# Layer-norm means on TensorE: one float32 product each, or two float32r products of an exact split

## The chip, the core and the metric

One of the cores of a Trainium2 chip runs the whole kernel, as one program in one launch. The metric is the device time of the execution in microseconds; the median of several runs counts. The engines are TensorE (PE in the profile; PEld is its weight load), VectorE (DVE), ScalarE (ACT), GpSimd (POOL) and SyncE (SP), which issues the DMAs.

## What is computed

One layer of a streaming encoder over 1024 prompt frames and 32 sample frames, 1056 columns of 1024 channels in all. Cut to the part that the change touches:

```python
def _layer_norm(x, g, b):
    mu = jnp.mean(xf, axis=-1, keepdims=True)
    var = jnp.mean(jnp.square(xf - mu), axis=-1, keepdims=True)
    y = (xf - mu) * lax.rsqrt(var + LN_EPS) * g + b
...
    mix = jnp.einsum('btd,de->bte', g_conv * y_conv + g_attn * y_attn, w_o)
    x1 = _layer_norm(DN_ALPHA * x + mix, ln1_g, ln1_b)
    h = jnp.square(jax.nn.relu(jnp.einsum('btd,df->btf', x1, w_up)))
    return _layer_norm(DN_ALPHA * x1 + jnp.einsum('btf,fd->btd', h, w_down), ln2_g, ln2_b)
```

Before these come a combined input projection, a convolution branch and an attention branch; their results and caches are outputs too.

## The kernel before

Channels lie on the 128 partitions, frames on the free axis, so the residual stream is eight tiles `acc[0..7]` of 128 x 1056, and a sum over channels is a sum over eight tiles followed by a sum over partitions. All large products run in float32r with operands that were split into two parts, hi and lo: a term is hi x hi + hi x lo + lo x hi, three products. A split is a Copy to float32r on ACT (hi) and a subtraction on DVE (lo).

**The norms.** `run_sum` adds the eight tiles of a block on DVE as they come. `norm_steps` (L1222) then takes the sum through the partitions with one product on PE whose weights are `mean_d`, a 128 x 128 tile filled with 1/1024 (L560); as both operands are float32 it is a float32 product. DVE subtracts the mean from each tile, ACT squares it, DVE adds the squares up (`squares`, L1200), and a second product with `mean_d` gives the variance. ACT takes the root, DVE the reciprocal, and `emit` writes each tile.

**Where they run.** The first norm (x1, behind w_o) is made in four blocks of 264 columns. The w_o products run in three groups: blocks 0 and 2, then block 1, then block 3 (`GROUPS`, L66). Its results, split into `x_0h`, `x_0l` to `x_3h`, `x_3l`, are what the first up-projection products read, in the order of blocks 0, 2, 1, 3 (`ORDER`, L67), four groups of 24 products for each block; inside a group the eight channel tiles are read one after the other, three products for each. Ahead of a block's first group `I.finish` (L1427) puts out what is left of its norm. The second norm (behind the down projection) is made in blocks of 384, 384 and 288 columns (`TAIL`, L63). The last block has a path of its own at the end of the kernel (L1790 on): it subtracts an estimate of the mean, the mean of its first tile times eight (`ps_mu_last`, copied by ACT to `lnpart`), as soon as that is there, while the other products run, and corrects it at the end; its products with `mean_d` are float32.

**What sets the order.** PE, DVE, ACT and POOL run their instructions in the order in which the program writes them. A planner (`class Issue`, L83) keeps an estimated clock for each engine while the program is written. After every six products of a large term, `service` (L127) looks at a list of background streams, the norms among them; each stream is a generator that yields what its next step needs, and it goes on when that is due by the clock of PE. A need with a number ahead of it, `(margin, need)`, is due that many ns after the need is ready; `NMARGIN` is 2000 (L73). A callable is due when it gives true: `yield lambda: nth < 2 or turned[nth - 2]` holds a norm back until the norm two before it has emitted its last tile. `("dve", "act", LAG)` lets a stream run at most 1 us ahead of PE.

```python
        margin = NMARGIN
        yield (margin, need)
        yield lambda: nth < 2 or turned[nth - 2]
        mu = cbank(f"mu_{tag}", "mu", 2)[:, :n]
        mean(mu, [s])
...
        yield (margin, [total])
        mean(var, [total])
```

Names in the trace: `lnsum_n` the sum, `lnsq_n` the squares, `lnvar_n` their sum, `ps_mu_n` and `ps_var_n` the two products, `rstd_n` the root and its reciprocal; `ps_o`, `ps_up` and `ps_dn` are the products of w_o, of the up projection and of the down projection. `spp` is the split of a hidden tile in the same stretch.

Of the kernel before, what the change touches and what calls it, by code (L numbers as in the profile page):

```python
# [9 lines left out]
F32 = mybir.dt.float32  # L10
F32R = mybir.dt.float32r
BF16 = mybir.dt.bfloat16
AF = mybir.ActivationFunctionType
# [4 lines left out]
P = 128  # L18
D = 1024
# [43 lines left out]
TAIL = (384, 384, 288)  # L63
CB = T // 4
# [18 lines left out]
class Issue:  # L83
# [121 lines left out]
    def mm(self, ps, w, x, start, stop):  # L205
        n = self.size(ps)
        self.run("pe", 122 if n == CB else max(107, n / 2.36) if x.dtype != F32 else max(430, n * 1.71), [ps], [w, x])
        self.nc.tensor.matmul(ps, lhsT=w, rhs=x, start=start, stop=stop)  # L208
# [5 lines left out]
    def act(self, out, in_, func, bias=None, **kw):  # L214
        aps = [] if bias is None else [bias]
        self.run("act", self.size(in_) * 0.81 + (62 if self.psum(in_) else 103) + 93 * len(aps),
                 [out] + [v for k, v in kw.items() if k == "accum_out"], [in_] + aps)
        if bias is not None:
            kw["bias"] = bias
        self.nc.scalar.activation(out, in_, func, **kw)  # L220
# [5 lines left out]
    def tt(self, out, a, b, op, eng="dve"):  # L226
        n = self.size(out)
        self.run(eng, n * 1.01 + 80 if eng == "dve" else n * 1.97 + 150, [out], [a, b])
        (self.nc.vector if eng == "dve" else self.nc.gpsimd).tensor_tensor(out, a, b, op)  # L229
# [31 lines left out]
def col(t, k):  # L261
    return t[:, k * P:(k + 1) * P]


def f32(t):
    return t.bitcast(F32)
# [3 lines left out]
def hybrid_layer(ctx: ExitStack, tc, io):  # L270
    nc = tc.nc
    I = Issue(nc)
    dma, mm, act, cp, tt, ts, stt = I.dma, I.mm, I.act, I.cp, I.tt, I.ts, I.stt
    ADD, SUB, MUL, MAX, MIN = ALU.add, ALU.subtract, ALU.mult, ALU.max, ALU.min

    @contextmanager
    def pool(name, **kw):
        with tc.tile_pool(name=name, bufs=1, reuse_waits="tile", **kw) as p:
            yield Slots(I, p)

    ctx.enter_context(tc.manual_schedule(engines={mybir.EngineType.PE, mybir.EngineType.DVE, mybir.EngineType.Activation, mybir.EngineType.Pool}))
    const = ctx.enter_context(pool("const"))
# [151 lines left out]
    def mm3(ps, terms, late=False, low=False):  # L434

        order = [(0, i, j) for i in range(len(terms)) for j in range(3)]
        if late:
            order.sort(key=lambda o: o[2] == 2)
        if low:
            order.sort(key=lambda o: o[2] == 1)  # L440
        n = len(order)
        for s, (_, i, j) in enumerate(order):
            wh, wl, xh, xl = terms[i]
            mm(ps, wl if j == 2 else wh, xl if j == 1 else xh, s == 0, s == n - 1)
            if s % (8 if low else 6) == (7 if low else 5) and s < n - 1:
                yield False
        yield True

    def dense(ps, terms, late=False):
        for _ in mm3(ps, terms, late):  # L450
            I.service()


    xp = ctx.enter_context(pool("x"))

# [39 lines left out]
    with pool("conv") as pv_, pool("a") as pa, pool("pa", space=PSUM) as psa:  # L495
# [61 lines left out]
        nc.gpsimd.memset(ones, 1.0)  # L557
        mean_c = pv_.tile([P, P], F32, name="mean_c")
        nc.gpsimd.memset(mean_c, 1.0 / C_CONV)
        mean_d = const.tile([P, P], F32, name="mean_d")  # L560
        nc.gpsimd.memset(mean_d, 1.0 / D)
        zt = pa.tile([P, 9, H], F32, name="zt")
        nc.gpsimd.memset(zt, 0.0)
        cum = pa.tile([P, 16, H], F32, name="cum")
# [179 lines left out]
        for half in range(2):  # L744
            ws = [W.take() for g in range(2)]
            for t in range(9):
                tk = slice(t * P, (t + 1) * P) if t < 8 else slice(T - P, T)
                ps = bank("v")[:, :VW]
# [6 lines left out]
                ps = ps[P - r:P, :]  # L755
# [20 lines left out]
        for m in range(4):  # L776
            for name in "qk":
                w = W.take()
                for c in range(NCH):
                    ps = bank(name)[:, :CH]  # L780
                    dense(ps, on_x(w, c))
                    a = pa.tile([P, CH], F32, tag="qk32", bufs=2, name=f"{name}32_{m}_{c}")
# [375 lines left out]
    pc = ctx.enter_context(pool("c"))  # L1158
    cblocks = [slice(b * CB, (b + 1) * CB) for b in range(NB)]
    num = [0]  # L1160
    bank_pool, ln_pool = [None], [None]

    def cbank(name, tag="acc", bufs=5):
        num[0] += 1
        return bank_pool[0].tile([P, 512], F32, tag=tag, bufs=bufs, name=f"ps_{name}_{num[0]}")
# [15 lines left out]
            return self.at(0, k), self.at(1, k)  # L1181

    def tmp(tag, bufs, name):
        return ln_pool[0].tile([P, LNW], F32, tag=tag, bufs=bufs, name=name)

    def run_sum(cs, m, s, tag, eng="dve"):

# [12 lines left out]
    def squares(sq, t, total, nth, n, tag):  # L1200

        m = len(sq)
        q = tmp(f"lnsq{nth % 2}", LNQ, f"lnsq{m}_{tag}")[:, :n]
        act(q, t, AF.Square)
        sq.append(q)
        if m == 2:
            total = tmp("lnvar", 2, f"lnvar_{tag}")[:, :n]
            tt(total, sq[0], sq[1], ADD)
        elif m > 2:
            tt(total, total, sq[m - 1], ADD)  # L1210
        return total

    def mean(ps, parts):
        for i, a in enumerate(parts):
            mm(ps, mean_d, a, i == 0, i == len(parts) - 1)
# [6 lines left out]
    def norm_steps(cs, tag, s, emit, need, nth):  # L1222
        n = cs.stop - cs.start
        tiles = [a[:, cs] for a in acc]
        margin = NMARGIN
        yield (margin, need)
        yield lambda: nth < 2 or turned[nth - 2]
        mu = cbank(f"mu_{tag}", "mu", 2)[:, :n]
        mean(mu, [s])
        var = cbank(f"var_{tag}", "var", 1)[:, :n]  # L1230
        total, sq = None, []
        for m, t in enumerate(tiles):
            tt(t, t, mu, SUB)
            total = squares(sq, t, total, nth, n, tag)
            if m % 2:
                yield ("dve", "act", LAG)
        tt(total, total, sq[-1], ADD)
        yield (margin, [total])
        mean(var, [total])
        rstd = tmp("lnrstd", 2, f"rstd_{tag}")[:, :n]  # L1240
        act(rstd, var, AF.Sqrt, bias=eps)
        I.recip(rstd, rstd)
        for m in range(KD):
            emit(m, rstd, tiles)
            turned[nth] = m == KD - 1
            yield ("dve", "act", LAG)

    with pool("ps1", space=PSUM) as bank_pool[0]:
        yo = [cbank("yo", "mu", 2)[:, :CB]]
        with pool("y") as py:  # L1250
# [27 lines left out]
            for n, (m, b) in enumerate(order):  # L1278
                if b == 0 and 0 < m < KD - 2:
                    load_gates(m + 2, py, 2)  # L1280
                while first and len(ahead) < (5 if n < YM * NB else 1):
# [3 lines left out]
                    ps = cbank("yc")[:, :CB]  # L1285
                    dense(ps, y_part(0, fm, cblocks[fb]))
                    ahead.append(ps)
                ps = yo.pop() if yo else cbank("yo", "mu", 2)[:, :CB]
# [18 lines left out]
        W.limit, W.engine = NPLAN, "dve"  # L1307
        S.pool = ctx_s.enter_context(pool("s", side="right"))
        with pool("l1") as ln_pool[0]:
            LNW, LNQ = CB, 2  # L1310
            for n, m in enumerate(m for m in range(0, KD, 2) if m not in WO_AGAIN):
                kept[NWO + m] = lambda n=n, m=m: [ln_pool[0].tile([P, T], F32R, tag=f"d{n}", bufs=2, name=f"{x}_wo{m}") for x in ("whi", "wlo")]
            xrs = []
# [56 lines left out]
            for group in GROUPS:  # L1370
                sums = {}
                for m in range(KD):
                    again = m in wk
                    w = wk[m] if again else W.take()
                    for b in group:
                        load_x(taken + 2)
                        taken += 1
                        ps = cbank("o")[:, :CB]
# [45 lines left out]
            for n, (f, b) in enumerate(order):  # L1424
# [9 lines left out]
                ps = cbank("up")[:, :CB]  # L1434
# [77 lines left out]
    with pool("ps2", space=PSUM) as psd:  # L1512
# [64 lines left out]
        for p in PAIRS:  # L1577
# [9 lines left out]
            ps = go(4)  # L1587
# [94 lines left out]
        for kb in range(NKB):  # L1682
            if kb == 1:
                extra = between()
            for g in range(2):
# [3 lines left out]
                for i in range(7):  # L1689
# [12 lines left out]
                    for n in range(2):  # L1702
                        q = 2 * g + n
                        ps = product(f"d{i}", [[(col(wh, 2 * n + f), col(wl, 2 * n + f), u[s][:, 2 * f * CB:(2 * f + 1) * CB],
                                                 u[s][:, (2 * f + 1) * CB:(2 * f + 2) * CB]) for f in range(2)] for s in range(2)])
# [22 lines left out]

    bank_pool[0] = ctx.enter_context(pool("ps3", space=PSUM))
    ln_pool[0] = ctx.enter_context(pool("l2"))  # L1730
    LNW, LNQ = max(TAIL), 3
    W.limit = len(plan)

    def output(cs, new=False):
# [45 lines left out]
    for i, cs in enumerate(tail):  # L1780
# [11 lines left out]
        n, s = cs.stop - cs.start, None  # L1792
        for m in range(KD):
            ps = more(m)
            a = acc[m][:, cs]
            tt(a, ps, a, ADD)
            s = run_sum(cs, m, s, f"n2_{i}")
# [4 lines left out]
    n, tag = cs.stop - cs.start, "n2_last"  # L1802
    tiles = [a[:, cs] for a in acc]
    nth, sq, var, s, held_ps = len(turned), [], None, None, {}
# [12 lines left out]
    for m in range(KD):  # L1817
        held_ps[m] = more(m)
        if m == 0:
            tt(tiles[0], held_ps.pop(0), tiles[0], ADD)  # L1820
            mu = cbank("mu_last", "mu", 2)[:, :n]
            part = spare("lnpart")
        if m == KM:
# [4 lines left out]
            s = spare("lnsum2")  # L1828
# [11 lines left out]
    ps = cbank("var_last", "var", 1)[:, :n]  # L1840
# [95 lines left out]
```

## Time and profile before

| | us |
|---|---|
| median of 3 runs | 1450.78 |
| lowest, highest | 1450.74, 1450.80 |
| the profiled execution | 1450.36 |
| its span, first to last instruction | 1448.6 |
| PE busy in the span | 1429.2 (99%) |
| DVE busy | 1122.0 (77%) |
| ACT busy | 678.8 (47%) |
| POOL busy | 127.0 (9%) |
| mean granted clock of TensorE | 0.995 of full speed |

The profile is of one execution, and its own time stands beside its span. An engine's busy share is a mean over stages with different limits, so what a change in one stage is worth is read from that stage: from the chain of work that ended last, and from the idle time ahead of an instruction with what ended it, which the timeline shows in brackets. PE's matmuls overlap: a row's duration is longer than the time by which it moves the next one, and that time is read from the chain or from the distance of starts.

### The profile page before, as it was taken

How to read it: one execution, taken by the hardware profiler on the slowest of the kernel's cores; microseconds unless marked ns; L12 is line 12 of the kernel's file. 1: busy time of each engine (PE TensorE's matmuls, PEld its weight loads, DVE VectorE, ACT ScalarE, POOL GpSimd, SP SyncE). 2: the span in 40 equal slices, each digit the busy share in tenths (PEclk: the TensorE clock that was granted, in tenths of full speed). 3: DMA queues.
4: the chain of work that ended last, by engine and by line, in shares of the span. 5: the costliest groups of instructions: out<-in, count | busy, mean ns of one | idle time of the engine just before them, and what ended most of it. 6: DMA issues, size and time to landing. Idle time of an engine off the chain costs nothing.

```text
span 1448.6 us, 28009 instructions
## 1 busy us (share of the span) xinstructions
PE 1429.2 (99%) x10639; PEld 1406.0 (97%) x10639; DVE 1122.0 (77%) x1926; ACT 678.8 (47%) x1426; POOL 127.0 (9%) x186
## 2 busy tenths in 40 slices
PE   9999999999999999999999999999999999999995
PEld 8999999999999999999999999999999999999994
DVE  6999899865666655856697889888985799879767
ACT  5113333455666656533345666666656332222224
POOL 0000000023455533000000000000000000000001
PEclk9999999999999999999999999999999999999997
DMA  7125554278455557426233347676689888884112
GB/s 247 46 61 160 165 171 159 90 244 234 111 150 157 153 153 263 147 78 195 86 127 128 133 171 281 237 253 239 229 301 335 331 315 313 295 314 161 46 44 77
DMA packets 157442, 267.91 MB, mean 185 GB/s; under 512 B 22680, under 2 KB 81272, under 8 KB 157308
## 3 DMA queue, kind: packets, MB, share of 16 engines
q1 hardware_dynamic: 156764, 264.54, 55.1%
q0 software_dynamic: 544, 1.59, 0.5%
q8 instruction: 84, 1.38, 0.4%
q14 instruction: 50, 0.41, 0.1%
HBM read 168.29 MB, written 97.74 MB: 184 GB/s over the span
## 4 chain that ended last, share of the span: by engine, by line
PE 96%; DVE 2%; ACT 1%; DMA 0%; issue 0%; SPq 0%; ACTq 0%; DVEq 0%
PE ps_u L208 18%; PE ps_d L208 17%; PE ps_g L208 13%; PE ps_o L208 6%; PE ps_dn L208 6%; PE ps_up L208 5%; PE ps_v L208 4%; PE ps_yc L208 3%; PE ps_k L208 3%; PE ps_glua L208 3%; PE ps_q L208 3%; PE ps_glub L208 3%; PE ps_yo L208 3%; PE ps_s L208 3%; PE ps_pv L208 2%; PE ps_tr L212 2%
## 5 line engine op out<-in xcount | busy, mean ns | idle before, releaser
L237 DVE SCALAR_TENSOR_TENSOR ca<-u,prm,ca 128x1086 f32<-128x1086 f32 x120 | 161.8, 1348 | 2.4
L208 PE MATMUL ps_g<-xh,whi 128*128 128x352 f32 x384 | 131.8, 343 | 0.0
L220 ACT ACTIVATE swhi<-s 128x512 fp32r<-128x512 f32 x100 | 61.9, 624 | 147.2 <-DVE s L229 140.7
L208 PE MATMUL ps_g<-xh,wlo 128*128 128x352 f32 x384 | 123.8, 322 | 0.0
L208 PE MATMUL ps_g<-xl,whi 128*128 128x352 f32 x384 | 121.5, 322 | 0.0
L208 PE MATMUL ps_u<-tl,swhi 128*128 128x264 f32 x416 | 118.4, 285 | 0.0
L208 PE MATMUL ps_u<-th,swhi 128*128 128x264 f32 x416 | 118.2, 284 | 0.0
L208 PE MATMUL ps_u<-th,swlo 128*128 128x264 f32 x416 | 118.2, 284 | 0.0
L220 ACT ACTIVATE whi<-raw 128x512 fp32r<-128x512 f32 (+1 forms) x120 | 69.7, 625 | 71.8 <-PE ps_glua L208 21.8
L229 DVE TENSOR_TENSOR tl<-ps_tr,th 128x512 fp32r<-128x512 f32 (+2 forms) x96 | 51.5, 553 | 60.1 <-ACT th L220 59.4
L208 PE MATMUL ps_d<-hu_h,swhi 128*128 128x264 f32 x480 | 93.0, 285 | 0.0
L208 PE MATMUL ps_d<-hu_l,swhi 128*128 128x264 f32 x480 | 92.8, 285 | 0.0
L220 ACT ACTIVATE r<-r 128x528 f32<-128x528 f32 (+1 forms) x120 | 73.9, 616 | 38.2 <-DVE r L229 35.9
L229 DVE TENSOR_TENSOR r<-r,ps_u 128x528 f32<-128x528 f32 x91 | 62.8, 702 | 29.9 <-PE ps_u L208 29.9
L229 DVE TENSOR_TENSOR wlo<-raw,whi 128x512 fp32r<-128x512 f32 (+1 forms) x100 | 64.8, 688 | 26.7 <-ACT whi L220 25.1
L229 POOL TENSOR_TENSOR acc<-acc,lnrest 128x288 f32<-128x288 f32 x5 | 3.8, 788 | 860.6 <-DVE lnvar_n_last L229 860.6
L208 PEld LDWEIGHTS ps_u<-th,swhi 128*128 128x128 f32 x416 | 78.3, 188 | 0.0
L208 PEld LDWEIGHTS ps_u<-th,swlo 128*128 128x128 f32 x416 | 78.3, 188 | 0.0
L208 PEld LDWEIGHTS ps_u<-tl,swhi 128*128 128x128 f32 x416 | 78.2, 188 | 0.0
L208 PEld LDWEIGHTS ps_d<-hu_h,swhi 128*128 128x128 f32 x480 | 74.6, 189 | 0.3 <-issue 0.2
L208 PEld LDWEIGHTS ps_d<-hu_l,swhi 128*128 128x128 f32 x480 | 74.6, 189 | 0.0
L208 PEld LDWEIGHTS ps_g<-xh,whi 128*128 128x128 f32 x384 | 72.7, 189 | 0.8
(423 smaller groups left out, 5008.7 us busy)
## 6 DMA issues: line engine op xcount, KB each, us to landing
h_s<-sp SPq DMA_DIRECT2D x84, 528.0 KB
raw<-in_w_in_dram SPq DMA_DIRECT2D x64, 256.0 KB
hu_h<-h_s SPq DMA_DIRECT2D x30, 528.0 KB
hu_l<-h_s SPq DMA_DIRECT2D x30, 528.0 KB
sraw<-in_w_up_dram SPq DMA_DIRECT2D x52, 256.0 KB
hu<-h_s SPq DMA_DIRECT2D x24, 528.0 KB
sraw<-in_w_ds_dram SPq DMA_DIRECT2D x48, 256.0 KB
g_s<-gt SPq DMA_DIRECT2D x48, 176.0 KB
```

Source lines behind the costliest of these rows:

```text
L208: self.nc.tensor.matmul(ps, lhsT=w, rhs=x, start=start, stop=stop)
L212: self.nc.tensor.transpose(ps, x, ident)
L220: self.nc.scalar.activation(out, in_, func, **kw)
L229: (self.nc.vector if eng == "dve" else self.nc.gpsimd).tensor_tensor(out, a, b, op)
L237: self.nc.vector.scalar_tensor_tensor(out, a, s, b, op0, op1)
```

## The change

Each sum is split in two before its product: hi is the sum rounded to float32r (a Copy on ACT), lo the rest (a subtraction on DVE). The mean is then two float32r products with the same weights, accumulated in one bank. The weights tile becomes float32r, `mean_r`, and `mean_d` is the same tile read as float32. The parts take slots of the tag of the squares. The wait for the sum comes without a margin now, the split follows, and the margin stands behind the parts. This holds for the norms that go through `norm_steps`: four blocks of the first norm and two of the second; the last block is as before.

```diff
+    def two_parts(src, pool, nth, tag):
+        n = src.shape[-1]
+        parts = [pool.tile([P, LNW[0]], F32R, tag=f"lnsq{nth % 2}", bufs=LNQ[0], name=f"ln{x}_{tag}")[:, :n] for x in "hl"]
+        act(parts[0], src, AF.Copy)
+        tt(parts[1], src, f32(parts[0]), SUB)
+        return parts
+
+    def mean_of(ps, share, parts):
+        for i, a in enumerate(parts):
+            mm(ps, share, a, i == 0, i == len(parts) - 1)
...
-        mean_d = const.tile([P, P], F32, name="mean_d")
-        nc.gpsimd.memset(mean_d, 1.0 / D)
+        mean_r = const.tile([P, P], F32R, name="mean_r")
+        nc.gpsimd.memset(f32(mean_r), 1.0 / D)
+        mean_d = f32(mean_r)
...
-        yield (margin, need)
+        yield need
         yield lambda: nth < 2 or turned[nth - 2]
+        parts = two_parts(s, ln_pool[0], nth, f"mu_{tag}")
+        yield (margin, parts)
         mu = cbank(f"mu_{tag}", "mu", 2)[:, :n]
-        mean(mu, [s])
+        mean_of(mu, mean_r, parts)
...
         tt(total, total, sq[-1], ADD)
-        yield (margin, [total])
-        mean(var, [total])
+        parts = two_parts(total, ln_pool[0], nth, f"var_{tag}")
+        yield (margin, parts)
+        mean_of(var, mean_r, parts)
```

The rest of the diff turns the width and the number of buffers of these tiles, `LNW` and `LNQ`, into one-element lists, with the same values.

## Rows read from the trace of the kernel before

**Rows 1.** The page, parts 1 and 4: busy shares, and the chain by engine.

```profile
PE 1429.2 (99%) x10639; PEld 1406.0 (97%) x10639; DVE 1122.0 (77%) x1926; ACT 678.8 (47%) x1426; POOL 127.0 (9%) x186
...
PE 96%; DVE 2%; ACT 1%; DMA 0%; issue 0%; SPq 0%; ACTq 0%; DVEq 0%
```

**Rows 2.** Waits of PE over the span, the longest: total, times, longest (us).

```profile
PE ps_md_last L208 <- DVE acc L229: 2.8, 1, 2.8
```

**Rows 3.** Chain in order of time, two stretches: start, length (us), what.

```profile
701.68 0.45 PE ps_mu_n L208 x2
...
702.12 2.91 PE ps_o L208 x24
...
1371.22 0.65 PE ps_mu_n L208 x2
...
1371.87 12.59 PE ps_dn L208 x72
```

**Rows 4.** Instructions that read mean_d: ns min/median/max, first and last start.

```profile
L208 PE MATMUL ps_mu_n<-lnsum_n,mean_d x12: 384/386/486, 701.5 to 1406.1; 128*128 128x264 f32 x8, 128*128 128x384 f32 x4
```

**Rows 5.** Instructions on spp, a split of the same width: ns min/median/max.

```profile
L220 ACT ACTIVATE spp<-r x20: 423/426/635, 763.4 to 1075.2; 128x264 fp32r<-128x264 f32 x16, 128x528 fp32r<-128x528 f32 x4
...
L229 DVE TENSOR_TENSOR spp<-r,spp x20: 426/431/711, 771.4 to 1078.6; 128x264 fp32r<-128x264 f32 x16, 128x528 fp32r<-128x528 f32 x4
```

**Rows 6.** Timeline of DVE, w_o and first w_up products: start, length (us).

```profile
701.44 0.43 DVE L229 TENSOR_TENSOR lnsum_n<-lnsum_n,acc 128x264 f32<-128x264 f32 x1
...
702.16 1.11 DVE L229 TENSOR_TENSOR acc<-acc,ps_mu_n 128x264 f32<-128x264 f32 x3 [0.28 <-PE ps_mu_n L208]
...
717.51 1.80 DVE L241 RECIPROCAL rstd_n<-rstd_n 128x264 f32<-128x264 f32 x1 [1.20 <-ACT rstd_n L220]
...
774.85 1.80 DVE L241 RECIPROCAL rstd_n<-rstd_n 128x264 f32<-128x264 f32 x1 [3.05 <-ACT rstd_n L220]
...
783.36 0.49 DVE L237 SCALAR_TENSOR_TENSOR x_3l<-acc,prm,x_3h 128x264 fp32r<-128x264 f32 x1 [0.18 <-ACT x_3h L220]
...
790.90 1.29 DVE L229 TENSOR_TENSOR wlo<-raw,whi 128x512 fp32r<-128x512 f32 x2 [4.76 <-ACT whi L220]
```

**Rows 7.** Timeline of ACT, same stretch.

```profile
715.70 1.28 ACT L220 ACT_TABLE_LOAD   x1
```

**Rows 8.** Timeline of PE, same stretch.

```profile
701.52 0.61 PE L208 MATMUL ps_mu_n<-lnsum_n,mean_d 128*128 128x264 f32 x2
...
785.78 0.28 PE L208 MATMUL ps_up<-x_3h,whi 128*128 128x264 f32 x1
...
788.34 0.28 PE L208 MATMUL ps_up<-x_3h,whi 128*128 128x264 f32 x1
```

**Rows 9.** Busy time by stretch: us, PE, PEld, DVE, ACT, POOL, PEclk, DMA.

```profile
721.00:741.00 20.00, 20.00 (x164) 19.87 (x163) 18.65 (x46) 9.20 (x20) 0.00 (x0) 1.00 0.48 150
...
750.00:760.00 10.00, 10.00 (x82) 9.87 (x81) 9.05 (x26) 5.87 (x15) 0.00 (x0) 1.00 0.36 121
...
1433.00:1434.50 1.50, 0.97 (x2) 0.50 (x2) 0.84 (x3) 1.50 (x4) 0.00 (x0) 0.50 0.92 330
```

**Rows 10.** Timeline of DVE, last block.

```profile
1402.57 0.56 DVE L229 TENSOR_TENSOR lnsum_n<-lnsum_n,acc 128x384 f32<-128x384 f32 x1
...
1406.61 1.48 DVE L229 TENSOR_TENSOR acc<-acc,ps_mu_n 128x384 f32<-128x384 f32 x3 [0.99 <-PE ps_mu_n L208]
...
1413.63 0.56 DVE L229 TENSOR_TENSOR lnvar_n<-lnvar_n,lnsq_n 128x384 f32<-128x384 f32 x1 [0.18 <-ACT lnsq_n L220]
...
1416.29 3.04 DVE L229 TENSOR_TENSOR acc<-acc,lnpart 128x288 f32<-128x288 f32 x8 [2.10 <-ACT lnpart L220]
```

**Rows 11.** Timeline of ACT and PE, last block.

```profile
1413.07 0.53 ACT L220 ACTIVATE lnsq_n<-acc 128x384 f32<-128x384 f32 x1 [0.41 <-DVE acc L229]
...
1415.85 0.41 ACT L220 ACTIVATE lnpart<-ps_mu_last 128x288 f32<-128x288 f32 x1 [2.25 <-PE ps_mu_last L208]
...
1405.77 0.81 PE L208 MATMUL ps_mu_n<-lnsum_n,mean_d 128*128 128x384 f32 x2
```

More of the change, by code (lines that the diff above doesn't have):

```diff
@@ L451, in dense @@
             I.service()
+    ln_pool, LNW, LNQ = [None], [0], [0]
     xp = ctx.enter_context(pool("x"))
@@ L1160, in hybrid_layer @@
     num = [0]
-    bank_pool, ln_pool = [None], [None]
+    bank_pool = [None]
     def cbank(name, tag="acc", bufs=5):
@@ L1183, in tmp @@
     def tmp(tag, bufs, name):
-        return ln_pool[0].tile([P, LNW], F32, tag=tag, bufs=bufs, name=name)
+        return ln_pool[0].tile([P, LNW[0]], F32, tag=tag, bufs=bufs, name=name)
     def run_sum(cs, m, s, tag, eng="dve"):
@@ L1202, in squares @@
         m = len(sq)
-        q = tmp(f"lnsq{nth % 2}", LNQ, f"lnsq{m}_{tag}")[:, :n]
+        q = tmp(f"lnsq{nth % 2}", LNQ[0], f"lnsq{m}_{tag}")[:, :n]
         act(q, t, AF.Square)
@@ L1309, in hybrid_layer @@
         with pool("l1") as ln_pool[0]:
-            LNW, LNQ = CB, 2
+            LNW[0], LNQ[0] = CB, 2
             for n, m in enumerate(m for m in range(0, KD, 2) if m not in WO_AGAIN):
@@ L1730, in hybrid_layer @@
     ln_pool[0] = ctx.enter_context(pool("l2"))
-    LNW, LNQ = max(TAIL), 3
+    LNW[0], LNQ[0] = max(TAIL), 3
     W.limit = len(plan)
```

## The prediction, made before the changed kernel ran

> **What bounds the kernel now.** The page's busy shares and its chain come first: TensorE (PE) is busy for 99% of the span and makes 96% of the chain that ended last, DVE 2%, ACT 1% [rows 1]. Then the waits of PE: the longest is 2.8 us, once, in the last norm [rows 2]. So until the last block's sums a product taken off PE shortens the run by its own length, unless something that feeds PE becomes late; after that DVE bounds. Next I read what the mean products take in the chain, and last the two places where work of DVE stands nearest to PE: the fourth block's x1 before the up projection, and the last block.
>
> **PE, what goes.** Six norms are touched (four blocks of 264 columns, two of 384), each with one product for the mean and one for the variance; the trace writes a float32 product as two matmuls, so its twelve rows for the mean, and as many for the variance, are 8 products of 264 and 4 of 384 together [rows 4]. In the chain one of 264 holds PE for 0.45 us, one of 384 for 0.65 us. An ordinary float32r product takes 2.91/24 = 0.121 us at 264 and 12.59/72 = 0.175 us at 384 [rows 3]. Two of these replace one: 0.45 - 0.24 = 0.21 us and 0.65 - 0.35 = 0.30 us saved. All twelve give 8 x 0.21 + 4 x 0.30 = 2.9 us, the most the change can give.
>
> [...]
>
> **What is added.** Each product gets a Copy to float32r on ACT and a subtraction on DVE: twelve of each. The same pair at 264 columns stands in the trace as spp: 0.42 us on ACT, 0.43 us on DVE [rows 5]; at 384 the nearest rows are 0.53 us and 0.56 us [rows 10, 11]. ACT, at 47% [rows 1], takes its share beside other work. Weights, DMAs and their queues stay as they are; memory too, since the parts take slots of the squares. The one memset is only renamed. What counts is order: the subtraction stands in DVE's queue behind older work, waits there for ACT with all younger work behind it, and the 2.0 us margin now runs from the parts, where it ran from the sum.
>
> **The x1 norms.** The first block's sum is old when its norm is set up, so its product went out at once, at 701.52 [rows 8]. Now its second part stands behind the other block's sum (701.44 + 0.43), is done at some 702.3, and the margin and the planner's step of six products (6 x 0.121 = 0.73 us) put the product at 704.4 to 705.1, so DVE's first subtraction of the mean moves from 702.16 [rows 6] to about 705.2. Of these 3.0 us most return: the next tile's residual work moves ahead, and DVE's 1.20 us of idle time before the first reciprocal [rows 6], most of which went by while ACT loaded a table (1.28 us, [rows 7]), shrinks if that load runs in ACT's new gap. I take 1.0 us late at the first reciprocal; 0 to 3.0 are the bounds.
>
> From there DVE has little room: 18.65 of 20 us and 9.05 of 10 busy [rows 9]. Five more DVE parts come before the fourth block's last x1 piece: 5 x 0.43 = 2.2 us; before three of them the sum is fresh, so DVE waits for ACT: 3 x 0.42 = 1.3 us. Of the idle time in the two stretches, 1.35 + 0.95 us, I let 1.0 be filled by work that is now deferred. The third and fourth norm also wait for the norm two before them, and only then split and start the margin; another norm's subtractions should fill that gap (cost 0; if that cover is gone, 2.0 us each). Lateness: 1.0 + 2.2 + 1.3 - 1.0 = 3.5 us, from 0 (all filled) to 3.0 + 3.5 + 4.0 = 10.5.
>
> The last piece of x1 of that block is done at 783.36 + 0.49 = 783.85 [rows 6]. Its first group on PE starts at 785.78, but reads that piece only with its 22nd product, at 788.34 [rows 8]: 4.5 us later. PE comes 8 x 0.21 = 1.7 us earlier, which leaves 2.8. So PE waits 3.5 - 2.8 = 0.7 us, from 0 to 7.7. Past it DVE idled for 4.76 us, up to 790.90, for weights that ACT had yet to split [rows 6]; that hides what is still late there, so I carry nothing on (without that cover up to 0.7 us more).
>
> **The feed-forward norms.** The first has a whole block of PE work over it; both savings count, 2 x 0.30. The second decides the tail. Its sum is done at 1402.57 + 0.56 = 1403.13 [rows 10], its product came at 1405.77 [rows 11]; the two parts add 0.53 + 0.56 = 1.1 us, with the planner's step (0.8 us at 288 columns) 1.1 to 1.9; I take two steps, 1.6. The shorter pair gives 0.3 back: the subtractions start 1.3 us late, and their chain ends at 1413.63 + 0.56 + 1.3 = 1415.5. The split of the variance sum follows, to 1416.6. The last block's subtractions began at 1416.29, after 2.10 us idle [rows 10], released by ACT's lnpart, which ended at 1415.85 + 0.41 [rows 11]. So they start 0.3 us later against the gains already made, and this norm's own savings are lost: its mean goes into that delay, its variance lies behind. Bounds: 0.3 us better, or 1.5 worse if three of its last multiplications (0.56 each in the like row) fall behind the last block's work.
>
> **Sum.** -1.7 - 0.6 + 0.3 + 0.7 = -1.3 us. The profiled execution took 1450.36 us (span 1448.6), 0.4 below the median of the runs, 1450.78; against the median 1449.5.
>
> **Rivals.**
> First, **all hidden**: DVE fills its gaps, PE never waits for x1. Then -1.7 - 0.6 with the tail between -0.3 and +0.3: -2.0 to -2.6, so 1448.2 to 1448.8. For it: the planner interleaves two norms, and 4.5 us is room. Against it: the DVE shares.
> Second, **x1 late, slower than before**: the lateness at the fourth block's x1 is the mechanism. From 4.8 us of it on, the wait (over 2.0 us) eats the gain, which is 2.0 us without it; at 6.5 us the run is 1.7 us slower, 1452.5; past 7.7 us it is slower by over 0.2%. For it: the two gated norms each now pay split and margin after their gate. Against it: there is another norm's work to run. PE would not sit still in it but do three products per arriving piece; the one longer wait in the trace, 2.8 us [rows 2], is followed by a granted clock of 0.50 (1.2 GHz) [rows 9], and that would be added.
> Third, **no shorter product**: if two float32r products with this weight hold PE as long as the float32 one, nothing is saved, the room at x1 stays 4.5 us and hides the lateness, and the tail loses 0.6: 1451.4. The cadence of all the neighbours speaks against it.
>
> **How the numbers follow.** Forecast with PE's wait between 0 and 2.0 us (1448.8 to 1450.8): 0.5. All hidden: 0.25. X1 late: 0.2, of which about 0.06 is slower by more than 0.2%. No shorter product: 0.05. 0.2% is 2.9 us, about what a measurement of this kernel can tell from no change; the ceiling lies there, so faster by more gets 0.03 (a happier order in the tail), slower 0.07, the same 0.90. The range drops the ends of rival two and of rival one: 1448.1 to 1452.3.
>
> **What would show it.** In the changed profile: mean products of 0.24 and 0.35 us in the chain; the first mean near 705 and not 701.5; x_3l's last write near 787 and a wait of PE for x_3l of some tenths of a us up to 2; the idle time of DVE before lnpart's subtractions gone from 2.10 to nearly 0. No wait of PE for x_3l would make the first rival true; one over 2 us the second; mean pairs of 0.45 us the third.

## The result, and the profile of the changed kernel

The changed kernel is slower: 1453.93 us in the median of 20 runs (1452.79 to 1456.16) beside 1450.80 for the kernel before, also of 20; the ratio is 1.0019, interval 1.0013 to 1.0025, so 1.9 to 3.6 us. The profiled execution took 1453.53 us, its span is 1451.3. Of the 2.7 us by which the spans differ, 0.45 lie ahead of the `ps_glub` product that starts at 31.53 us in the trace before (the first of its long group of 72): that start moves between the profiles (31.4 to 32.9 us over all kernels here), so every difference below is counted from that product; this is what "start-up taken out" means. Net of it the change costs 2.25 us in the trace. The medians differ by 3.1 us. Some 0.4 of that lie outside the span: the time beyond it is 2.2 us in the mean of these 20 runs and 1.8 in the runs of the kernel before, and why is not shown.

The page, parts 1 and 4, against [rows 1]:

```profile
PE 1429.7 (99%) x10639; PEld 1407.4 (97%) x10639; DVE 1127.9 (78%) x1938; ACT 683.3 (47%) x1438; POOL 127.1 (9%) x186
...
PE 95%; DVE 3%; ACT 1%; DMA 0%; issue 0%; ACTq 0%; SPq 0%; DVEq 0%
```

DVE and ACT have twelve instructions more each, PE as many as before: the twelve means and variances are two matmuls each either way, but shorter. DVE's share of the chain has grown from 2 to 3%. The waits of PE, longest first (total, times, longest), show where:

```profile
PE ps_md_last L208 <- DVE acc L229: 3.3, 1, 3.3
...
PE ps_up L208 <- ACT x_3h L220: 1.0, 1, 1.0
...
PE ps_up L208 <- DVE x_3l L237: 0.2, 1, 0.2
```

The last two are new; the first lies in the drain at the end, behind PE's last long group of products. The chain around the first norm (start, length, what):

```profile
705.16 0.25 PE ps_mu_n L208 x2
...
762.13 17.43 PE ps_up L208 x144
779.56 0.26 PE ps_var_n L208 x2
...
779.84 0.49 ACT rstd_n L220
...
780.35 1.81 DVE rstd_n L241
...
784.13 2.50 DMA hp_s<-spp
...
786.71 0.42 ACT spp L220
787.14 0.41 ACT x_3h L220
...
787.57 0.51 DVE x_3l L237
...
788.12 0.80 PE ps_up L208 x3
...
788.93 35.04 PE ps_up L208 x275
```

A pair of mean products holds PE for 0.25 us where one product held it for 0.45 [rows 3]. But the chain leaves PE at the variance of the fourth block's norm and comes back only at 788.12, over the root, the reciprocal and the writing of x1. DVE in that stretch, against [rows 6]:

```profile
720.71 1.80 DVE L241 RECIPROCAL rstd_n<-rstd_n 128x264 f32<-128x264 f32 x1 [1.20 <-ACT rstd_n L220]
...
780.35 1.80 DVE L241 RECIPROCAL rstd_n<-rstd_n 128x264 f32<-128x264 f32 x1 [1.86 <-ACT rstd_n L220]
...
787.57 0.49 DVE L237 SCALAR_TENSOR_TENSOR x_3l<-acc,prm,x_3h 128x264 fp32r<-128x264 f32 x1 [0.80 <-ACT x_3h L220]
...
790.67 0.49 DVE L237 SCALAR_TENSOR_TENSOR x_3l<-acc,prm,x_3h 128x264 fp32r<-128x264 f32 x1 [0.18 <-ACT x_3h L220]
...
794.23 1.29 DVE L229 TENSOR_TENSOR wlo<-raw,whi 128x512 fp32r<-128x512 f32 x2 [1.77 <-ACT whi L220]
```

The last x_3l ends at 791.16, before at 783.85: 6.86 us later, start-up taken out. PE, against [rows 8], had arrived earlier:

```profile
784.74 0.28 PE L208 MATMUL ps_up<-x_3h,whi 128*128 128x264 f32 x1
...
786.30 0.28 PE L208 MATMUL ps_up<-x_3h,wlo 128*128 128x264 f32 x1
787.59 0.39 PE L208 MATMUL ps_up<-x_3h,whi 128*128 128x264 f32 x1 [1.01 <-ACT x_3h L220]
```

784.74 is 1.49 us earlier than 785.78 net of start-up. The first `ps_u` product, the next hand-over, before and after:

```profile
820.63 0.28 PE L208 MATMUL ps_u<-x_0h,swhi 128*128 128x264 f32 x1
823.80 0.28 PE L208 MATMUL ps_u<-x_0h,swhi 128*128 128x264 f32 x1
```

The way from the first product with x_3h to it took 34.85 us before (785.78 to 820.63) and after 4.21 more: that distance, less 34.85, is called **the wait** below, since a wait spread over many short gaps doesn't show whole in the list of waits. From that product to DVE's first subtraction of lnpart it is 0.27 us less, and from there to the end 0.20 less. So -1.49 + 4.21 - 0.27 - 0.20 = +2.25 us: the whole loss of the trace is the wait at the fourth block's x1. (The 0.20 is no effect of the change that can be told: over the kernels below this last stretch is 0.38 us shorter to 0.18 longer, and 0.38 shorter in one whose feed-forward norms are as before.)

The end has gained as forecast. DVE in the last block, against [rows 10]:

```profile
1418.72 0.56 DVE L229 TENSOR_TENSOR lnl_var_n<-lnvar_n,lnh_var_n 128x384 fp32r<-128x384 f32 x1 [0.59 <-ACT lnh_var_n L220]
1419.19 3.03 DVE L229 TENSOR_TENSOR acc<-acc,lnpart 128x288 f32<-128x288 f32 x8
```

The idle time of 2.10 us ahead of lnpart's subtractions is gone.

### The profile page after: what moved, and what is told of

It reads as the page before. It is cut to its first block, busy times and chain, and to the rows that moved or that the text cites. A ratio compares the mean times of both kernels' runs of the same rounds, so it can differ in the third digit from the quotient of the medians.

```text
span 1451.3 us, 28041 instructions
## 1 busy us (share of the span) xinstructions
PE 1429.7 (99%) x10639; PEld 1407.4 (97%) x10639; DVE 1127.9 (78%) x1938; ACT 683.3 (47%) x1438; POOL 127.1 (9%) x186
## 4 chain that ended last, share of the span: by engine, by line
PE 95%; DVE 3%; ACT 1%; DMA 0%; issue 0%; ACTq 0%; SPq 0%; DVEq 0%
PE ps_u L208 18%; PE ps_d L208 17%; PE ps_g L208 13%; PE ps_o L208 6%; PE ps_dn L208 5%; PE ps_up L208 5%; PE ps_v L208 4%; PE ps_glub L208 3%; PE ps_yc L208 3%; PE ps_k L208 3%; PE ps_glua L208 3%; PE ps_q L208 3%; PE ps_yo L208 3%; PE ps_s L208 3%; PE ps_pv L208 2%; PE ps_tr L212 2%
```

## The experiments

Four explanations of the late x1 were set against each other. **Work**: DVE has the parts to make on top of a queue that was nearly full. **Waits**: the products of the mean and of the variance go out later, since the margin runs from the parts and, for the third and fourth norm, starts only after their gate. **A hold on ACT**: the split of a hidden tile (`spp`) stands ahead of x_3h and waits for a DMA. **The number of norms**: how many of the four are split, and which. The quoted texts use short names: theory A is that the loss is PE's wait for the fourth block's x1, A1 the hold on ACT, A3 the waits, A4 the work. "Late" is the end of the last x_3l against before, start-up taken out. It still holds what PE had lost ahead of the first norm, where nothing was changed (at the w_o product that starts at 690.12 us before): 0.90 us in pool_x1, 0.63 in pool_due, 0.57 in pool_all_but_last, 0.39 in wait_only and work_only, 0.12 in the changed kernel, at most 0.15 in the others.

**Which half of the change.** The norms are counted by `nth`: 0 to 3 are blocks 0, 2, 1, 3 of x1, 4 and 5 those of the feed-forward side. A norm goes the changed way if a condition holds, else the way of before (the variance likewise):

```diff
+        if nth >= 4:
             yield need
...
             mean_of(mu, mean_r, parts)
+        else:
+            yield (margin, need)
...
+            mean(mu, [s])
```

> The split only in the two feed-forward norms, float32 products in the four x1 norms as before. Theory A (the loss is PE's wait for the fourth block's x1): the x1 stage is as before, no wait of PE for x_3l, and the run gains the 0.6 us of the first feed-forward norm less some 0.3 to 0.5 at the last block: 0 to 0.5 us faster than before, ratio 0.9997 to 1.0000. Rival B (the tail loses too, by the delayed second norm): slower than before by 0.5 us or more.

Measured: 1.0004 (0.9995 to 1.0013); late 0.14, no wait. DVE's first subtraction of lnpart comes 0.28 us earlier, and the stretch from it to the end is 0.18 us longer.

With `nth < 4` in its place:

> The split only in the four x1 norms. Theory A: PE waits about 4.2 us in the fourth block's first group as in the changed kernel (from its first product with x_3h to the first ps_u 39.1 us against 34.9), less 1.6 saved on eight products: 2.6 us slower than before, ratio about 1.0018. Rival B: half of the loss or less, since the tail makes the rest.

Measured: 1.0021 (1.0012 to 1.0029); late 6.88, wait 4.81. So the x1 norms make the loss. (0.80 us of x1_only's loss lie elsewhere: PE waits 0.6 us at a product of `ps_d` at 1293 us.) What the feed-forward norms do by themselves the times leave open: the median of ffn_only is 0.6 us above the kernel before, and the interval holds no change as well as rival B's 0.5 us. In the trace their gain at lnpart is the 0.28 us that was forecast.

**The hold on ACT.** In the changed kernel ACT stood still ahead of x_3h (its timeline):

```profile
786.71 0.42 ACT L220 ACTIVATE spp<-r 128x264 fp32r<-128x264 f32 x1 [1.04 <-DMA hp_s<-spp]
787.04 0.91 ACT L220 ACTIVATE x_3h<-acc,prm 128x264 fp32r<-128x264 f32 x2
```

This kernel puts the pending hidden tiles' splits at another place in that stretch:

```diff
-                if len(pending) > 1:
+                keep = 0 if n == 7 else 2 if 8 <= n < 12 else 1
+                while len(pending) > keep:
                     rest()
```

> The changed kernel with the hidden tiles' splits (spp) moved out of the time in which the fourth block's x1 is written: one is made ahead, two behind. Theory A1 (the hold of ACT by these splits and by their buffer, which waits for a DMA, is a part of the lateness): x_3l's last write 2 to 2.5 us earlier, PE's wait 4.2 down to about 2, the run 2 us faster than the changed kernel. Rival A2 (the lateness is already there when the fourth reciprocal ends, and DVE sets the pace after it): less than 1 us earlier, the run within 1 us of the changed kernel.

Measured: 1.0024 (1.0015 to 1.0033); late 7.19, wait 3.47. PE lost another 0.73 us ahead of that distance, since its first product with x_3h already stood still (0.59 us idle), so it waited for x1 as long as in the changed kernel. A miss: the hold only changed place, and what the run would do without it stays untested. ACT now stands before the variance's first part, and DVE behind it (timelines of ACT and of DVE):

```profile
780.56 0.42 ACT L220 ACTIVATE spp<-r 128x264 fp32r<-128x264 f32 x1 [1.58 <-DMA hp_s<-spp]
...
781.16 0.41 ACT L220 ACTIVATE lnh_var_n<-lnvar_n 128x264 fp32r<-128x264 f32 x1
```

```profile
781.61 0.43 DVE L229 TENSOR_TENSOR lnl_var_n<-lnvar_n,lnh_var_n 128x264 fp32r<-128x264 f32 x1 [2.13 <-ACT lnh_var_n L220]
```

The fourth reciprocal is 7.26 us late, where it was 5.05, and what the writing of x1 gained went there.

**The margin.** Back to the sum for the mean; the parts have none:

```diff
-        yield need
+        yield (margin, need)
...
-        yield (margin, parts)
+        yield parts
```

> The changed kernel with the margin of the mean's product counted from the sum again, the split behind it, and the product due as soon as the parts are; the variance as in the changed kernel. Theory A3 (the restarted margin is a large part of the lateness): first mean product near 702 instead of 705, those of the third and fourth norm 2 us earlier, x_3l's last write 2 to 3 us earlier, the run 2 to 3 us faster than the changed kernel. Rival A4 (the split's own work and waits on DVE are the lateness): x_3l less than 1 us earlier, and perhaps short waits of PE for the parts.

The variance keeps its margin behind the parts. Measured: 1.0015 (1.0006 to 1.0024); late 6.93, wait 3.63. Nothing gained at x1: the first mean came 1.5 us earlier than in the changed kernel, the second 2.9 later.

**Waits alone, work alone.** First the kernel before with float32 products and no parts, but each x1 product held until PE's planned clock reaches the time at which the parts and their margin would be over (cut to the mean; the variance likewise):

```diff
+            hi_at = max(I.ready(s, "act"), I.t["act"]) + n * 0.81 + 103 + 130
+            due_mu = max(hi_at, I.t["dve"]) + n * 1.01 + 80 + 130 + margin
+            yield lambda: I.t["pe"] >= due_mu
```

> The kernel before, with no split at all, but the x1 norms' eight float32 products held back until the planner's time at which the changed kernel's parts and margin would be due. Theory A4 (the split's own work and waits on DVE are the lateness, 6.7 us at x_3l's last write): less than 3 us of lateness against the kernel before, and no wait of PE (its room is 4.5 us). Rival A3 (the restarted margin is the lateness): 4 us or more.

Measured, in one run: 1451.98 us beside 1451.12; late 5.53, wait 0.68. Then the parts made but unread in the x1 norms, the float32 products at the due times of before (the variance likewise):

```diff
-        yield need
+        yield (margin, need)
...
-        parts = two_parts(s, ln_pool[0], nth, f"mu_{tag}")
-        yield (margin, parts)
+        if nth < 4:
+            two_parts(s, ln_pool[0], nth, f"mu_{tag}")
...
-        mean_of(mu, mean_r, parts)
+        mean(mu, [s])
```

> The changed kernel with the splits of the x1 norms made but unused: their products stay float32 and are due as before the change (the margin from the sum; the feed-forward norms are also float32 and without a split). Theory A4: lateness of x_3l's last write of 4 us or more against the kernel before, PE's wait small, since PE has not gained 1.6 us: 0 to 1.5 us. Rival A3: less than 3 us of lateness.

Measured, in one run: 1456.27 us; late 8.84, wait 5.16. So both explanations hold and neither rules the other out: each alone uses up the room of 4.5 us, the distance from the last x_3l to the product that needs it, which is worked out further down. They don't add up: 5.53 and 8.84 alone, 6.86 together. Held products leave idle time on DVE that parts can fill: ahead of the fourth reciprocal 4.25 us in wait_only, 1.86 in the changed kernel. That this is why they don't add up is argued and not tested by itself.

**The second part on POOL**, which is idle in this stretch:

```diff
-        tt(parts[1], src, f32(parts[0]), SUB)
+        tt(parts[1], src, f32(parts[0]), SUB, "pool" if nth < 4 else "dve")
```

> The changed kernel with the x1 norms' subtractions on POOL, which does nothing there. Theory A4: DVE loses eight parts (2.8 us busy) and four waits for ACT (2.3 us); x_3l's last write comes 3 to 5 us earlier than in the changed kernel, PE's wait of 4.2 us falls to 1 or less, and the run is 3 us faster than the changed kernel, 0 to 1 us faster than before. Rival A3: POOL's subtraction is slower (0.7 to 0.8 us), the products come later still, and x_3l less than 1 us earlier.

Measured: 0.9995 (0.9987 to 1.0004); late 4.45, wait 0.72. With DVE rid of eight subtractions the wait is nearly gone, with the change's rule for the due times in place. What the eight Copies on ACT cost by themselves no run takes apart. The next has the part of the first feed-forward norm on POOL too, and the second feed-forward norm as before (`nth < 5` in both places):

> As the run with POOL, and the first feed-forward norm's subtractions on POOL too; the second feed-forward norm as before the change, float32 and without a split. Theory A4: gains of 1.6 us and 0.6 us stand, less up to 1 us of wait: 1 to 2.2 us faster than before, ratio 0.9985 to 0.9993. Rival: the tail's start gives nothing back, and the run is as before.

Measured: 0.9991 (0.9982 to 1.0000); late 4.12, wait 0.73. In the x1 norms the two kernels are the same, and less what PE had lost ahead of the first norm (0.90 and 0.57) both are 3.55 late. POOL's timeline in the first of the two:

```profile
700.67 0.75 POOL L229 TENSOR_TENSOR lnl_mu_n<-lnsum_n,lnh_mu_n 128x264 fp32r<-128x264 f32 x1 [124.75 <-ACT lnh_mu_n L220]
...
737.75 0.90 POOL L229 TENSOR_TENSOR lnl_var_n<-lnvar_n,lnh_var_n 128x264 fp32r<-128x264 f32 x1 [2.83 <-ACT lnh_var_n L220]
```

A part takes POOL 0.76 us where DVE takes 0.43, and one of the eight took 0.90.

With the parts of the same five norms on POOL, the margins were then run from the sums again, so that the parts get none (cut to the mean; the variance likewise):

```diff
+            yield (margin, need)
...
+            parts = two_parts(s, ln_pool[0], nth, f"mu_{tag}")
+            yield parts
```

> As the last run with POOL (subtractions of five norms on POOL, the sixth norm as before the change), with the margins counted from the sums again and the products due as soon as the parts are. The theory now (two causes, either of which uses up the room: the split's work on DVE, and the products' later due time): both are gone, x_3l's last write at most 2.8 us late (4.1 in the run with POOL alone), no wait of PE (0.7 there), so 2.2 us faster than before, ratio 0.9985. Rival (the rest of the lateness is the chain ACT, POOL, PE, ACT behind each variance sum, and no due time): x_3l 3.5 us or more late, the run as with POOL alone.

Measured: 0.9998 (0.9989 to 1.0007); late 4.98, no wait at x1, but PE arrives there 0.89 us later than before and not earlier. The forecast, at most 2.8 us late and 2.2 us faster, missed. PE was 0.63 us late ahead of the first norm; the shorter products should have turned that into 1.0 us early, so 1.9 us went in between, most of it at the products themselves (waits of PE):

```profile
PE ps_mu_n L208 <- POOL lnl_mu_n L229: 0.7, 1, 0.7
...
PE ps_mu_n L208 <- ACT lnh_mu_n L220: 0.3, 1, 0.3
```

So the margin is not waste: without it PE, in order, stands before a part that isn't there.

**How many norms, and which.** The condition of the first experiment with other sets, the feed-forward norms as before. The first two of x1 (`nth < 2`):

> The split, as in the changed kernel, only in the first two x1 norms; the other four norms as before. If lateness adds up norm by norm (the split's work on DVE throughout the stage): x_3l's last write 2.5 to 4 us late, about half of 6.9, and inside the room of 4.5 - 0.8 = 3.7 us, so PE waits 0 to 0.5 us and the run is 0.3 to 0.8 us faster than before, ratio 0.9994 to 0.9998. If the fourth norm's own parts are what comes late (its chain is the last): less than 1.5 us late.

Measured: 0.9997 (0.9988 to 1.0006); late 1.36, no wait. The last two of x1 (`nth in (2, 3)`):

> The split, as in the changed kernel, only in the third and fourth x1 norms (blocks 1 and 3); all others as before. The first two alone made x_3l 1.4 us late, all four 6.9 us. If the two halves add up: 5.5 us late, room 4.5 - 0.8 = 3.7 us, so PE waits about 1.8 us and the run is 1.0 us slower than before. If the halves only together pass a threshold (DVE full because all four split): less than 3.7 us late, no wait, 0.8 us faster than before.

Measured: 0.9992 (0.9983 to 1.0001); late 3.31, no wait. The fourth alone (`nth == 3`):

> The split only in the fourth x1 norm (block 3). If its own chain, gate, split, margin, and again split and margin, is the lateness: 3 us or more at x_3l's last write. If the third norm's chain ahead of it on DVE and ACT is: less than 2 us. Room 4.5 - 0.4 = 4.1 us: no wait of PE in either case, the run within 0.5 us of before.

Measured: 0.9995 (0.9986 to 1.0004); late 3.77, no wait. Three of x1, without the first (`nth in (1, 2, 3)`) and without the second (`nth in (0, 2, 3)`), one run each:

> The split, as in the changed kernel, in the second, third and fourth x1 norms (blocks 2, 1, 3); the first as before, and the feed-forward norms as before. If the first norm's late start is what makes all four together later than the halves: 3.3 to 4.3 us late at x_3l, room 4.5 - 1.2 = 3.3, PE waits 0 to 1 us. If it is the number of splits on a full DVE: 5 us or more, PE waits 1.7 us or more.

> The split in the first, third and fourth x1 norms (blocks 0, 1, 3); the second as before, and the feed-forward norms as before. If the first norm's late start is the cause: 5 us or more late at x_3l, PE waits 1.7 us or more. If it is the number of splits: about as without the first.

Measured: late 4.07 and 3.93, waits 0.69 and 0.73, times 1451.81 and 1450.12 beside 1451.01. The two texts read these outcomes in opposite ways: 4.07 fits the first norm's late start as the cause, 3.93 speaks against it, and neither explanation covers both. The first of these times holds a wait of 0.7 us of another product, `ps_d` near 1105 us, for ACT; first_two (0.8) and pool_due (0.7) have such a wait there too, while the changed kernel, without_second and pool_all_but_last have none.

The timeline of PE tells what the split of a norm does. Starts of the products, before, and how much later (us, start-up taken out):

| product | before | after | first_two | last_two | fourth_only | wait_only | work_only |
|---|---|---|---|---|---|---|---|
| mean, 1st norm | 701.52 | +3.03 | +2.99 | +0.06 | +0.10 | +3.31 | +0.39 |
| variance, 2nd | 737.44 | +2.21 | +3.09 | -0.14 | +0.10 | +1.85 | +3.30 |
| mean, 3rd | 729.72 | +5.34 | +0.95 | +2.98 | +0.10 | +6.21 | +0.41 |
| variance, 3rd | 758.70 | +2.57 | +1.50 | +0.36 | -0.12 | +1.83 | +4.10 |
| mean, 4th | 753.88 | +2.76 | -0.70 | +2.74 | +3.00 | +4.75 | +1.16 |
| variance, 4th | 773.69 | +5.25 | +0.80 | +3.06 | +3.52 | +4.75 | +7.02 |

In last_two the third norm's mean is 2.98 late and its variance 0.36: 29 us lie between the two, in which DVE works for the fourth block as well, and the lateness is made up. The fourth norm, the last, makes up nothing: its mean is 3.00 late in fourth_only and its variance 3.52. With all four split the third norm's mean is 5.34 late and the fourth's variance 5.25. A late start of the third norm is not enough for that: in without_second its mean is 6.17 late and the fourth's variance 3.34.

**The best set without POOL.** The last two of x1 and the first of the feed-forward side (`nth in (2, 3, 4)`):

> The split, as in the changed kernel, in the third and fourth x1 norms and the first feed-forward norm; the three others as before. The third and fourth x1 norms alone were 3.3 us late at x_3l, inside the room, with no wait of PE and 0.8 us gained there. If the gains of norms that nothing waits for add up: 0.8 + 0.6 = 1.4 us faster than before, ratio 0.9990, lnpart's subtractions 1.4 us earlier. Rival: the first feed-forward norm's saving is lost behind the second's, as the tail gained only 0.2 us in the run with five norms on POOL: 1.0 us faster, ratio 0.9993.

Measured: 0.9993 (0.9984 to 1.0002); late 3.28, no wait, PE at x1 0.83 earlier, lnpart's subtractions 0.59 earlier still: 1.42 us less than before in the trace. The last x_3l write, and the cover behind it (DVE's timeline):

```profile
786.90 0.49 DVE L237 SCALAR_TENSOR_TENSOR x_3l<-acc,prm,x_3h 128x264 fp32r<-128x264 f32 x1 [0.18 <-ACT x_3h L220]
790.80 1.29 DVE L229 TENSOR_TENSOR wlo<-raw,whi 128x512 fp32r<-128x512 f32 x2 [1.77 <-ACT whi L220]
```

This kernel and pool_all_but_last are faster than the changed one, since their intervals against before don't touch its own; that either beats the kernel before by 0.1% is what the trace says, and the times can't settle it.

**The clock in the wait.** The wait should be the lateness less the room, and the room is 4.49 us [rows 6, 8] plus the time by which PE arrives later (less, if earlier). That gives 0.64, 0.67, 0.68, 0.65, 0.67, 3.43 and 3.58 us for wait_only, pool_x1, pool_all_but_last, without_first, without_second, spp_moved and margin_sum, where 0.68, 0.72, 0.73, 0.69, 0.73, 3.47 and 3.63 were measured. In three kernels it falls short: 3.86 for 4.21 in the changed one, 3.87 for 4.81 in x1_only, 3.88 for 5.16 in work_only. There the granted clock had dropped. Busy time by stretch in the changed kernel (us, PE, PEld, DVE, ACT, POOL, PEclk, DMA), against [rows 9]:

```profile
786.00:787.00 1.00, 0.51 (x2) 0.30 (x2) 0.77 (x3) 0.29 (x1) 0.00 (x0) 1.00 0.90 305
787.00:788.00 1.00, 0.39 (x1) 0.19 (x1) 0.43 (x2) 0.95 (x3) 0.00 (x0) 1.00 0.38 127
788.00:789.00 1.00, 0.87 (x4) 0.56 (x4) 1.00 (x4) 0.49 (x1) 0.00 (x0) 0.71 0.82 279
789.00:790.00 1.00, 1.00 (x4) 0.91 (x5) 1.00 (x3) 0.54 (x2) 0.00 (x0) 0.50 0.39 135
790.00:791.00 1.00, 1.00 (x5) 0.91 (x6) 0.82 (x3) 0.52 (x1) 0.00 (x0) 0.50 0.47 158
791.00:792.00 1.00, 1.00 (x7) 1.00 (x7) 1.00 (x3) 0.00 (x0) 0.00 (x0) 0.58 0.35 120
792.00:793.00 1.00, 1.00 (x10) 1.00 (x10) 0.47 (x1) 0.89 (x2) 0.00 (x0) 1.00 0.00 0
```

PE is back at full work at 789, but at 0.50 (1.2 GHz), four to five matmuls a us and not ten, until shortly before 792. That the lower clock is what lengthens the wait in these three kernels is read from the two facts together, the excess and the clock; in the seven others the clock stayed at 1.00 in this stretch.

## Why the prediction failed, step by step

It said 1449.5 us, between 1448.1 and 1452.3, and named the mechanism that came as its second rival: x1 late, slower than before. The likeliest case had the same mechanism with a wait of 0.7 us; what failed is the size of the lateness, 3.5 us forecast and 6.86 measured. The result lies 4.4 us above the forecast. The wait, 0.7 forecast and 4.2 measured, makes 3.5 of them; some 0.4 lie outside the span, and 0.45 in the start-up of the two profiles, whose share in the medians is not known.

**PE's savings: right.** 0.24 to 0.26 us for a pair in the chain at 264 columns. At 384 the chain shows

```profile
1375.44 0.35 PE ps_mu_n L208 x2
1375.79 14.69 PE ps_dn L208 x84
1390.48 0.35 PE ps_var_n L208 x2
```

and 0.35 was forecast. PE arrives at x1 1.49 us earlier, 1.61 counted from the start of the x1 stage (1.7 by the forecast's terms); so it does in pool_x1 (1.61) and pool_all_but_last (1.62), and with fewer norms split by 0.43 (two products, fourth_only) to 1.27 us (six, without_second).

**The first mean: right; the first reciprocal: wrong.** 704.55 net of start-up, forecast 704.4 to 705.1. Of the 3.0 us most were to return, 1.0 left at the first reciprocal; 2.75 were left. The table load did not move into ACT's gap (ACT's timeline):

```profile
718.90 1.28 ACT L220 ACT_TABLE_LOAD   x1
720.20 0.48 ACT L220 ACTIVATE rstd_n<-ps_var_n,eps 128x264 f32<-128x264 f32 x1
```

It stands behind the last squares and right ahead of the root, as before, and DVE idles the same 1.20 us. At the fourth block both first norms together cost 1.36 us of lateness (first_two).

**The gated norms: the step that failed.** "Another norm's subtractions should fill that gap (cost 0; if that cover is gone, 2.0 us each)". The cover was there for the third norm and not for the fourth, which is the last: its mean comes 3.00 us late, its variance 3.52, and x1 3.77 (fourth_only). By the forecast's other terms this norm's two parts cost 2 x 0.43 and one wait for ACT, 0.42, together 1.3; so the gate's term measures some 2.5 us in fourth_only and not 0. With it the sum would have been 6.0 us late, the wait 3.2 and the forecast 1452.0, near the top of the range and still below the result. The 2.0 us named for a lost cover was short as well: the split, too, stands behind the gate. The 0.9 us between 6.0 and 6.86 come with all four norms split, and the next two points show where they lie, not what sets them off.

**Idle time filled: wrong in sign.** 1.0 us of DVE's idle time was to be filled. From the sum at 701.44 [rows 6] (702.01 after) to the last x_3l, DVE is busy for 76.78 us and not 72.82 (2.7 of the difference are eight parts at 0.34 us each), and idle for 12.37 and not 9.59. Work and idle time grew together: 4.0 + 2.8 = 6.7 us. (The gate's term is a part of this idle time, so the two are not to be added.) Part of that idle time is the third norm's root, which stands on ACT behind squares and hidden tiles (ACT and DVE in the changed kernel):

```profile
765.07 0.42 ACT L220 ACTIVATE spp<-r 128x264 fp32r<-128x264 f32 x1
765.40 0.46 ACT L220 ACTIVATE rstd_n<-ps_var_n,eps 128x264 f32<-128x264 f32 x1
```

```profile
765.90 1.81 DVE L241 RECIPROCAL rstd_n<-rstd_n 128x264 f32<-128x264 f32 x1 [1.62 <-ACT rstd_n L220]
```

The variance product was at 761.72, so it is 3.7 us from product to root, where before it was 0.7 (PE and ACT before, PE after):

```profile
758.70 0.61 PE L208 MATMUL ps_var_n<-lnvar_n,mean_d 128*128 128x264 f32 x2
759.43 0.46 ACT L220 ACTIVATE rstd_n<-ps_var_n,eps 128x264 f32<-128x264 f32 x1
```

```profile
761.72 0.28 PE L208 MATMUL ps_var_n<-lnh_var_n,mean_r 128*128 128x264 f32 x1
```

**Not thought of: hidden tiles between the pieces of x1.** The fourth reciprocal is 5.05 us late and the last piece 6.86: writing the sixteen tiles took 9.01 us and not 7.20. In it DVE makes two hidden tiles' splits where it made one before (0.34 us each), and ACT the one that waited for a DMA (0.80 us of idle time on DVE).

**The room: right; the clock: named, not priced.** 2.8 us of room were forecast, 3.00 were there. (The 22nd product, from which the forecast counted, reads the last x_3h; the last x_3l is read by the 23rd, 0.12 us later.) By the account above the lower clock added 0.35 us in the changed kernel, and up to 1.28 in work_only. Nothing was carried on past x1, as said: DVE's idle time before the weights shrank from 4.76 to 1.77 us.

**The tail: right at lnpart.** 0.3 us earlier at lnpart's subtractions was forecast (-0.6 + 0.3); 0.27 in the changed kernel, 0.28 in ffn_only. More multiplications behind the last block's work were the bound; seven stand in the last group (1432.70) where six did. Behind lnpart's subtractions the end is 0.20 us shorter in the changed kernel and 0.18 longer in ffn_only, so no gain or loss can be read there.

**Still open.** The two sets of three x1 norms are 3.9 and 4.1 us late and all four 6.9. The third norm's reciprocal shows some of the 2.9 us between them (5.52 us late with all four, 3.37 and 1.27 in without_second and without_first), and so do the hidden tiles; why it takes the fourth split norm to bring them about was not settled. A third buffer for the hidden tiles' split, which would take away ACT's hold, was not tried.

## What to carry to other kernels

A cheaper instruction on the engine that bounds is worth its saving only if the work that pays for it, on other engines, stays inside the room at the next hand-over: measure that room (here 4.5 us) from the profile, and price the lateness by each norm's own successor, since cover that the third of four has is missing for the last. Where a margin starts behind a gate, and not beside it, its whole length and the split's count as latency. Take the saving where the room is (three late norms, or the parts on an idle engine) and leave the rest as it is.

## What the runs showed of the hardware that was not expected

PE's clock fell after a wait in pieces: in the changed kernel, x1_only and work_only PE did products as x_3l pieces came, its one longest idle time there was 1.0 us, and the granted clock fell to 0.50 (1.2 GHz) for some 3 us afterwards, with PE busy without a break. In spp_moved and margin_sum PE lost 4.2 and 3.6 us at the same place, but no single idle time was above 0.6 us, and the clock stayed at 1.00. Which of the two decides, the one idle time of 1.0 us or the load around it, no run here tells.

POOL and DVE slowed each other at some places only. Seven of POOL's eight parts in pool_x1 took 0.75 to 0.77 us and one 0.90, and beside that one (737.75) three of DVE's subtractions took 1.10 us, as three did in the kernel before (1.11, [rows 6]). In pool_due three of the eight took 0.86, 1.02 and 1.03 us, the last two while DVE made a `wlo` of 512 columns, and beside two of the three a sum of squares on DVE took 0.65 us where it takes 0.43. The Trainium skill, "GPSIMD Engine Reference", section "8. Key points", says that POOL shares its SBUF interfaces with DVE and contends with DVE instructions that read two tensors from SBUF. The long parts agree with that (`wlo` and the sum `lnsum_n` beside the others read two); the part at 756.42 in pool_x1 took 0.76 us beside such an instruction (`lnvar_n`), and no run here tries it by itself.
